# Time mixing: the modulation tiles move from the shared weight ring to three buffers of their own, loaded two tiles ahead

## The chip, the cores and the metric

The program runs on one core of a Trainium2 chip, in one launch. The metric is the device time of one execution in microseconds (us). It is given as the median of three runs.

## The reference, cut to what matters

The program is a small two-layer network on 256 positions of width 2048, all in f32. Layer 0 is RWKV-7 time mixing and an MLP; then one shared K and V are projected; layer 1 is banded attention and an MLP. Every sub-layer is normalised, scaled, shifted and gated by vectors that are computed from one condition vector `c`:

```python
mod = c @ w_ada[layer] + b_ada[layer]              # (1, 12288): 2048 x 12288 weights
sh1, sc1, gt1, sh2, sc2, gt2 = jnp.split(mod, 6, axis=-1)
h = modulate(rms_norm(x, g_mix[layer]), sh1, sc1)
y = rwkv7_time_mix(h, ...)                         # layer 0 only
x = x + gt1[:, None, :] * y
h = modulate(rms_norm(x, g_mlp[layer]), sh2, sc2)
x = x + gt2[:, None, :] * sq_relu_mlp(h, w_up[layer], w_down[layer])
```

The change concerns where the weights `w_ada` of `mod` lie while they are used. No result depends on it.

## The kernel before

**Weights.** Each 2048-wide product reads its f32 weights from HBM in tiles of 128x1024 (512 KB). `raw()` (L372) loads a tile on SyncE's queue into one of `RAW_BUFS` = 6 buffers named `raw`, which are used in turn (**the ring**): a load waits until the tile six loads back has been split. `halves()` splits a tile in two: ScalarE writes the rounded half `wH` (L382), VectorE the rest `wL` (L385); each has three buffers. TensorE multiplies by both halves (L405 to L407, or L416 and L418 in pairs). `weight_part` (L393) does the same with part of a tile.

**Modulation.** A part of `mod` (2048 numbers) is made in two halves of 16 tiles of `w_ada`. `ada_load` loads a tile; `ada_step` uses it on VectorE: the first tile of a half starts the accumulator `acc` (L458), each later one is added to it, times a number of `c` for each partition (L460). After the sixteenth, `ada_sum` adds `acc` up over the partitions by small matmuls (L482) and VectorE adds the bias (L486, `mod`). There is one buffer for `acc`. Where such a tile lies is decided here:

```python
def raw(self, src, shape=None, ada=False):
    if ada and self.ada_pool:
        pool, n = self.ada_pool
        t = pool.tile([P, HK * P], F32, tag="rada", bufs=n, name="rada")
    else:
        t = self.wp.tile([P, HK * P], F32, tag="raw", bufs=self.RAW_BUFS, name="raw")

def ada_fill(self):
    while self.ada_pool and len(self.ada_q) < self.ada_pool[1] - 1 and self.ada_load():
        pass
```

`ada_room(n)` opens a pool of n buffers named `rada` (in the MLPs n is 5, in the attention 3). While one is open, tiles of `w_ada` go there, `ada_fill` keeps n-1 of them ahead of their use, and when the room is left, `ada_drain` uses up what was loaded. Before, time mixing has no such room: there each `ada()` loads a tile into the shared ring and uses it at once.

**Time mixing.** The part of `layer_a` from L842 on runs 16 pairs of heads. A new pair begins every 8 slots, each has 36 steps (a chain of small dependent operations on all engines), and the loop over slots (L898 on) issues one step of each live pair, and two pieces of the dense products with `w_k` and `w_r` (L856 on), or of `w_o` at the end. From slot 16 on, three slots of four also call `ada()`: 111 tiles in all. Then `out_proj` multiplies by `w_o`: for each tile pair, VectorE adds the products to `x` (L955), scales the result (L557), and GpSimd adds up the squares (L524; the last is VectorE's). It reads `x` again from HBM (L941). The MLP's first products begin at once on rows that are not normalised yet, and `rstd()` (L530 on TensorE, L532 and L537 to L539 on VectorE) makes the norm beside them, which `late_norm` (L571, L572) multiplies in. L547 and L549 make the normalised rows for the rest of the MLP.

**Order.** The text of the program does not fix the order of the instructions by itself. A scheduler places each instruction on its engine by its own estimate of when its inputs are ready; an engine then runs its instructions strictly in the order that results. So a buffer more can move instructions far from the place of the edit. SyncE issues all large loads, in order, and waits at each for its buffer to be free.

Of the kernel before, what the change touches and what calls it, by code (L numbers as in the profile page):

```python
# [333 lines left out]
class Body:  # L334
# [305 lines left out]
    def layer_a(self, st, sp):  # L640
        nc, tc, d = self.nc, self.tc, self.d
# [199 lines left out]
        with ExitStack() as s1:  # L841
            pw = self.pw = s1.enter_context(tc.tile_pool(name="pw", bufs=1, reuse_waits="tile"))  # L842
            pp = self.pp = sp.enter_context(tc.tile_pool(name="ps_b", bufs=1, space=bass.MemoryType.PSUM,
                                                         reuse_waits="tile"))
            self.psm = lambda: pp.tile([P, 512], F32, tag="ms", bufs=2, name="ms")
            self.bones = pw.tile([P, P], F32R, name="bones")
            nc.scalar.copy(self.bones, self.cst("bones"))
            e01 = [pw.tile([P, 4, C + 1], F32, name=f"e01_{i}") for i in range(2)]
            self.uf = [pw.tile([P, 4, C], F32, name=f"uf_{i}") for i in range(2)]
            for e, u in zip(e01, self.uf):  # L850
                nc.vector.memset(e[:, :, 0:1], 1.0)  # L851
                nc.gpsimd.memset(u, 0.0)

            pairs = [Pair(self, j, v[:, j, :], tw, ta, tg, e01[j % 2]) for j in range(NPAIR)]

            def proj_steps(pr):  # L856
                for dst, hl in (("k", xk), ("r", xr)):
                    w = self.wnext
                    src = next(weights, None)
                    self.wnext = None if src is None else self.weight(src)  # L860
                    ps = pp.tile([P, 2 * T], F32, tag="pj", bufs=2, name="pj")[:, :T]
                    for kt in range(KT):
                        self.proj(ps, w, lambda kt: hl[:, kt, :, 0:T], (kt, kt + 1))
                        if dst == "r" and kt == 1:
                            pr.lw = pw.tile([P, 2, P], F32, tag="lw", bufs=1, name="lw")
                            nc.sync.dma_start(out=pr.lw, in_=d["lora2"][pr.j, :, 0:2])
                        if kt % 2 == 1:
                            if kt == KT - 1:
                                t = pw.tile([P, T], F32, tag=dst, bufs=2, name=dst)
                                nc.scalar.copy(t, ps)  # L870
                                setattr(pr, dst, t)
                            yield

            def out_steps():

                for n in range(8):
                    self.split(self.y_hl, n, v[:, n, :])
                sums, todo = self.o_ps, [(n, 0, HK) for n in range(8)] + [(n, HK, KT - 2) for n in range(4)]
                for n, lo, hi in todo:
                    if n % 2 == 0 and lo == 0:  # L880
                        tag = ("pj", "pj", "gr", "iv")[n // 2]
                        ps = pp.tile([P, 2 * T], F32, tag=tag, bufs=1 + (tag == "pj"), name="o")
                        sums.append(ps.rearrange("p (i t) -> p i t", i=2))
                    if lo == HK and n == 0:
                        assert all(p.done for p in pairs[:KT - 2])
                        for j in range(HK, KT - 2):
                            self.split(self.y_hl, j, v[:, j, :])
                    w = self.weight_part(d["w_o"][n], lo, hi)
                    for kt in range(lo, hi, 2):
                        self.proj(sums[n // 2][:, n % 2, :], w, lambda kt: self.y_hl[:, kt, :, 0:T],  # L890
                                  (kt, kt + 2), n % 2 == 0, False)
                        yield

            self.o_ps = []
            S, OUTS = self.SLOTS, 44
            inverts = range(Pair.EARLY, Pair.EARLY + Pair.INVERT)
            outs, done, n_out = None, 0, 0
            for slot in range(S * NPAIR + Pair.STEPS):  # L898
                live = []
                for j, pr in enumerate(pairs):  # L900
                    at = slot - S * (j + 1)
                    if 0 <= at < Pair.STEPS:
                        if at == 0:
                            pr.gen = pr.steps()
                        sums = at == Pair.STEPS - 3
                        live.append((0 if at in inverts else 1 + (at < Pair.EARLY) + 2 * sums, -at, pr))
                        pr.done = at == Pair.STEPS - 1
                last = self.last_pe()
                for _, _, pr in sorted(live, key=lambda x: x[:2]):
                    with tc.issue_after(last):  # L910
                        next(pr.gen)
                    last = self.last_pe()
                if slot < S * NPAIR:
                    if slot % S == 0:
                        dense = proj_steps(pairs[slot // S])
                    todo = 16 // S
                else:
                    if outs is None:
                        self.y_hl = self.new_hl()
                        outs = dense = out_steps()  # L920
                    todo = OUTS * (slot + 1 - S * NPAIR) // Pair.STEPS - n_out
                    n_out += todo
                with tc.issue_after(last):
                    for _ in range(todo):
                        next(dense, None)
                if slot >= 2 * S and slot % 4 < 3:
                    self.ada()
            self.fin(HK)
# [294 lines left out]


def build(arrays):
    nc = _bacc.Bacc("TRN2", target_bir_lowering=False, num_devices=1)
    d = {n: nc.dram_tensor(n, a.shape, F32, kind="ExternalInput").ap() for n, a in arrays.items()}
    d["out"] = nc.dram_tensor("out", (P, KT, T), F32, kind="ExternalOutput").ap()
    with tile.TileContext(nc) as tc, ExitStack() as ctx:
        Body(ctx, tc, d).run()  # L1230
    if not nc.is_finalized():
        nc.finalize()
    return nc
# [8 lines left out]
```

## Time and profile before

| | before |
|---|---|
| runs | 2661.66, 2654.56, 2652.42 us, median 2654.56 |
| profiled execution, first to last instruction | 2653.8 us |
| granted TensorE clock, mean | 0.993 |
| VectorE, ScalarE, GpSimd busy | 79%, 52%, 8% |

The page lists busy times, the queues, the chain of work that ended last, and the costliest groups of instructions. The time of the profiled execution itself is not listed; its span can be set beside the runs. Time mixing's pairs lie between about 185 and 710 us, `out_proj` and the start of MLP 0 between 710 and 815 us, the rest of MLP 0 up to about 1450 us. An instruction's row has line, engine, operation, and its output and inputs by the program's names; the idle time before it and what ended that idle time stand behind. TensorE's busy time has to be read with care: its matmuls are pipelined, and one of 128x256 lasts 0.28 us in a row while the next begins 0.12 us after it.

### The profile page before, as it was taken

Reading aid. Unit: us, or ns where it says so; the run is one execution under the profiler, and the core shown is the slowest. Engines: PE = TensorE matmul, PEld = TensorE weight load, DVE = VectorE, ACT = ScalarE, POOL = GpSimd, SP = SyncE. Lnnn points to the kernel's source line nnn. Section 1 sums busy time; section 2 is a strip of 40 time slices with the busy share of each in tenths; the row PEclk is TensorE's granted clock in tenths of the full one; section 3 lists DMA queues with packets and bytes.
Section 4 is the critical chain, followed back from the end, with each engine's and each line's share of the span. In section 5 each row is a group of like instructions: output and inputs, shape, how many; then the busy total and the mean of one; then the engine's idle time right before and its main releaser. Section 6 shows DMA issues by size and latency. Waiting matters only on the chain.

```text
span 2653.8 us, 59231 instructions
## 1 busy us (share of the span) xinstructions
PE 2574.9 (97%) x24108; PEld 2257.3 (85%) x24108; DVE 2089.4 (79%) x3054; ACT 1368.6 (52%) x2484; POOL 210.6 (8%) x338
## 2 busy tenths in 40 slices
PE   7999999999999999999999999999999999999997
PEld 4788888887899888888888998887898888888886
DVE  6888878878789888888888898899887556555555
ACT  3346555555456445355365554565564464453554
POOL 1002223223110000000001000000100000000002
PEclk9999999999999999999999999999999999999999
DMA  9976656565768888989888779887766555555553
GB/s 351 320 243 220 211 181 196 180 197 196 253 234 301 325 320 320 329 325 334 325 328 293 237 247 326 313 282 263 266 216 236 191 186 188 190 187 188 189 189 121
DMA packets 207664, 663.19 MB, mean 250 GB/s; under 512 B 21408, under 2 KB 55072, under 8 KB 207392
## 3 DMA queue, kind: packets, MB, share of 16 engines
q1 hardware_dynamic: 205328, 656.89, 71.7%
q8 instruction: 189, 3.10, 0.5%
q10 hardware_dynamic: 2064, 2.53, 0.3%
q14 instruction: 83, 0.68, 0.1%
HBM read 657.23 MB, written 2.10 MB: 248 GB/s over the span
## 4 chain that ended last, share of the span: by engine, by line
PE 84%; DVE 7%; issue 4%; DMA 3%; ACT 2%; POOL 1%; SPq 0%; DVEq 0%; ACTq 0%; POOLq 0%
PE pj L416 42%; PE pj L418 21%; PE pj L405 3%; PE pj L406 3%; PE pj L407 3%; DMA raw<-w_ada 2%; DVE wL L385 2%; DVE acc L460 1%; PE iv L111 1%; PE o L405 1%; PE ms L328 1%; PE o L407 0%; ACT wH L382 0%; PE o L406 0%; PE pT L1130 0%
## 5 line engine op out<-in xcount | busy, mean ns | idle before, releaser
L385 DVE TENSOR_TENSOR wL<-raw,wH 128x1024 fp32r<-128x1024 f32 x772 | 941.1, 1220 | 342.4 <-ACT wH L382 337.2
L382 ACT CAST wH<-raw 128x1024 fp32r<-128x1024 f32 x772 | 806.0, 1045 | 762.7 <-PE pj L416 590.2
L416 PE MATMUL pj<-aHL,wH 128*128 128x512 f32 x2816 | 893.3, 398 | 1.1 <-DVE x L955 1.1
L416 PE MATMUL pj<-hHL,wH 128*128 128x512 f32 x2048 | 644.7, 396 | 0.0
L418 PEld LDWEIGHTS pj<-aHL,wL 128*128 128x128 f32 x2816 | 531.7, 189 | 123.1 <-issue 0.3
L418 PE MATMUL pj<-aHL,wL 128*128 128x256 f32 x2816 | 564.1, 281 | 0.0
L418 PEld LDWEIGHTS pj<-hHL,wL 128*128 128x128 f32 x2048 | 384.5, 188 | 91.1 <-DVE wL L385 0.9
L416 PEld LDWEIGHTS pj<-aHL,wH 128*128 128x128 f32 x2816 | 432.1, 189 | 8.6 <-issue 8.3
L418 PE MATMUL pj<-hHL,wL 128*128 128x256 f32 x2048 | 402.6, 278 | 0.4 <-DVE wL L385 0.4
L460 DVE SCALAR_TENSOR_TENSOR acc<-rada,ct,acc 128x1024 f32<-128x1024 f32 x256 | 327.3, 1278 | 7.3 <-DMA rada<-w_ada 6.9
L416 PEld LDWEIGHTS pj<-hHL,wH 128*128 128x128 f32 x2048 | 312.2, 189 | 1.3 <-DVE hHL L1001 1.1
L405 PE MATMUL pj<-aHL,wH 128*128 128x256 f32 (+1 forms) x896 | 262.5, 293 | 0.0
L406 PE MATMUL pj<-aHL,wH 128*128 128x256 f32 (+1 forms) x896 | 254.2, 284 | 0.0
L407 PE MATMUL pj<-aHL,wL 128*128 128x256 f32 (+1 forms) x896 | 253.0, 282 | 0.0
L524 POOL TENSOR_TENSOR ss<-ss,sq 128x256 f32<-128x256 f32 x56 | 51.2, 915 | 1583.7 <-ACT sq L523 1583.4
L1026 DVE SCALAR_TENSOR_TENSOR x<-pj,mod,x 128x256 f32<-128x256 f32 x256 | 123.3, 482 | 64.2 <-PE pj L418 61.2
L405 PEld LDWEIGHTS pj<-aHL,wH 128*128 128x128 f32 x896 | 169.9, 190 | 4.5 <-issue 0.2
L407 PEld LDWEIGHTS pj<-aHL,wL 128*128 128x128 f32 x896 | 170.4, 190 | 0.4 <-DVE e L851 0.2
L406 PEld LDWEIGHTS pj<-aHL,wH 128*128 128x128 f32 x896 | 169.9, 190 | 0.5
L460 DVE SCALAR_TENSOR_TENSOR acc<-raw,ct,acc 128x1024 f32<-128x1024 f32 x104 | 138.0, 1327 | 17.4 <-DMA raw<-w_ada 17.2
L998 ACT ACTIVATE t<-t 128x256 f32<-128x256 f32 x112 | 46.9, 419 | 120.2 <-DVE t L970 120.2
L1001 DVE TENSOR_TENSOR hHL<-t,hHL 128x256 fp32r<-128x256 f32 x128 | 53.9, 421 | 1.7 <-ACT t L1000 1.0
(252 smaller groups left out, 2817.6 us busy)
## 6 DMA issues: line engine op xcount, KB each, us to landing
raw<-w_up SPq DMA_DIRECT2D x256, 512.0 KB, 4.0
raw<-w_down SPq DMA_DIRECT2D x256, 512.0 KB, 3.6
rada<-w_ada SPq DMA_DIRECT2D x209, 512.0 KB, 5.5
raw<-w_ada SPq DMA_DIRECT2D x111, 512.0 KB, 4.3
rada<-w_ada_kv SPq DMA_DIRECT2D x64, 512.0 KB, 6.6
rawa<-w_ada SPq DMA_DIRECT2D x32, 512.0 KB, 6.7
rawa<-w_ada_t SPq DMA_DIRECT2D x32, 512.0 KB, 7.1
raw<-w_k SPq DMA_DIRECT2D x32, 512.0 KB, 3.6
```

Of the source, the lines that this page charges most:

```text
L382: nc.scalar.copy(Hf, raw)
L385: eng.tensor_tensor(out=Lf, in0=raw, in1=Hf, op=ALU.subtract)
L405: nc.tensor.matmul(ps, H[:, i, :], a(kt)[:, 0, :], start=(first and kt == 0), stop=False)
L406: nc.tensor.matmul(ps, H[:, i, :], a(kt)[:, 1, :], start=False, stop=False)
L407: ins = nc.tensor.matmul(ps, L[:, i, :], a(kt)[:, 0, :], start=False, stop=(last and kt == KT - 1))
L416: nc.tensor.matmul(ps, w[kt // HK][0][:, kt % HK, :], a(kt), start=(kt == 0), stop=False)
L418: ins = nc.tensor.matmul(ps[:, 0, :], w[kt // HK][1][:, kt % HK, :], a(kt)[:, 0, :], start=False, stop=(kt == KT - 1))
L460: nc.vector.scalar_tensor_tensor(out=self.acc, in0=raw, scalar=ck, in1=self.acc, op0=ALU.mult, op1=ALU.add)
L524: (eng or nc.gpsimd).tensor_tensor(out=self.ss, in0=self.ss, in1=sq, op=ALU.add)
L998: nc.scalar.activation(t, t, AF.Relu)
L1001: nc.vector.tensor_tensor(out=h[:, 1, :], in0=t, in1=h[:, 0, :], op=ALU.subtract)
L1026: nc.vector.scalar_tensor_tensor(out=x, in0=ps[:, i, :], scalar=self.mods[(layer, 5)][:, n:n + 1], in1=x, op0=ALU.mult, op1=ALU.add)
```

## The change

A room of three buffers is opened around the loop over slots, and filled with two tiles at slot 12, four slots before the first `ada()`. When it is left, the two tiles that are still loaded are used: 113 tiles instead of 111. The room comes from the scratch that the build reserves for dynamic DMAs, which is set to 1024 bytes. Below L854 the line numbers are one higher than before, below L927 three higher (L955 becomes L958, L941 becomes L944).

```diff
+            s1.enter_context(self.ada_room(3))
             pairs = [Pair(self, j, v[:, j, :], tw, ta, tg, e01[j % 2]) for j in range(NPAIR)]
...
+                if slot == 2 * S - 4:
+                    self.ada_fill()
                 if slot >= 2 * S and slot % 4 < 3:
                     self.ada()
...
-    nc = _bacc.Bacc("TRN2", target_bir_lowering=False, num_devices=1)
+    nc = _bacc.Bacc("TRN2", target_bir_lowering=False, num_devices=1, dynamic_dma_scratch_size=1024)
```

GpSimd's order is the same in both programs, and TensorE's but for a batch of L482. On VectorE, ScalarE and SyncE the orders differ from shortly before the first pair up to the beginning of MLP 0; from there to the end they are equal. Three places follow; a name's number tells one buffer's use from the next.

**SyncE, where the first pairs begin.** The weights of `w_r` and `w_k` are loaded for pairs 0 and 1. Before:

```order
L372 DMA raw_2220<-w_k 128x1024
L372 DMA raw_2226<-w_k 128x1024
L372 DMA raw_2291<-w_r 128x1024
L372 DMA raw_2297<-w_r 128x1024
L372 DMA raw_2389<-w_k 128x1024
L866 DMA lw_2239<-lora2 128x256
L281 DMA lg_3772<-lora2 128x256
L372 DMA raw_2395<-w_k 128x1024
L372 DMA raw_2513<-w_r 128x1024
L372 DMA raw_2519<-w_r 128x1024
L866 DMA lw_2408<-lora2 128x256
L372 DMA raw_2538<-w_ada 128x1024
```

After:

```order
L372 DMA raw_2160<-w_r 128x1024
L372 DMA raw_2166<-w_r 128x1024
L372 DMA rada_2419<-w_ada 128x1024
L372 DMA raw_2223<-w_k 128x1024
L372 DMA rada_2421<-w_ada 128x1024
L372 DMA raw_2229<-w_k 128x1024
L372 DMA rada_2547<-w_ada 128x1024
L372 DMA raw_2294<-w_r 128x1024
L372 DMA rada_2589<-w_ada 128x1024
L372 DMA rada_2635<-w_ada 128x1024
L372 DMA raw_2300<-w_r 128x1024
```

Before, the first tile of `w_ada` is loaded behind the weights of the third projection, in the same ring. Now the tiles stand between the weights, some ten rows earlier, and take no place in the ring.

**VectorE and SyncE in out_proj.** These are the last four pairs of tiles of `w_o`. VectorE before:

```order
L557 SCALAR_TENSOR_TENSOR aHL_11661<-x_11625,gain_g_mlp0_11631,aHL_11661 128x256
L385 TENSOR_TENSOR wL_12022<-raw_12019,wH_12021 128x1024
L460 SCALAR_TENSOR_TENSOR acc_11149<-rada_12294,ct_68,acc_11149 128x1024
L955 SCALAR_TENSOR_TENSOR x_11625<-pj_11966,mod_0_2_70,x_11625 128x256
L385 TENSOR_TENSOR wL_12076<-raw_12073,wH_12075 128x1024
L955 SCALAR_TENSOR_TENSOR x_11625<-pj_11966,mod_0_2_70,x_11625 128x256
L385 TENSOR_TENSOR wL_12082<-raw_12079,wH_12081 128x1024
L557 SCALAR_TENSOR_TENSOR aHL_11661<-x_11625,gain_g_mlp0_11631,aHL_11661 128x256
L955 SCALAR_TENSOR_TENSOR x_11625<-pj_12012,mod_0_2_70,x_11625 128x256 x2
```

VectorE after:

```order
L557 SCALAR_TENSOR_TENSOR aHL_11706<-x_11670,gain_g_mlp0_11676,aHL_11706 128x256
L460 SCALAR_TENSOR_TENSOR acc_11660<-rada_12339,ct_68,acc_11660 128x1024
L385 TENSOR_TENSOR wL_12067<-raw_12064,wH_12066 128x1024
L460 SCALAR_TENSOR_TENSOR acc_11660<-rada_12341,ct_68,acc_11660 128x1024
L958 SCALAR_TENSOR_TENSOR x_11670<-pj_12011,mod_0_2_70,x_11670 128x256
L385 TENSOR_TENSOR wL_12121<-raw_12118,wH_12120 128x1024
L958 SCALAR_TENSOR_TENSOR x_11670<-pj_12011,mod_0_2_70,x_11670 128x256
L385 TENSOR_TENSOR wL_12127<-raw_12124,wH_12126 128x1024
L557 SCALAR_TENSOR_TENSOR aHL_11706<-x_11670,gain_g_mlp0_11676,aHL_11706 128x256
L460 SCALAR_TENSOR_TENSOR acc_11660<-rada_12343,ct_68,acc_11660 128x1024
L958 SCALAR_TENSOR_TENSOR x_11670<-pj_12057,mod_0_2_70,x_11670 128x256
L385 TENSOR_TENSOR wL_12167<-raw_12164,wH_12166 128x1024
```

MLP 0's room of five buffers is open here already. Before, one tile of `w_ada` is added here, the last of the seventh half, and the next comes in MLP 0. Now the additions begin at the same place and come in every few rows. The reason lies in the count: 113 is 7 times 16 and 1, so the seventh half (tiles 97 to 112) is complete within time mixing, and the next half has begun in `acc`. Before, 111 tiles left the seventh half one short; its last tile is the one above, and the next half could begin only after that half's sum (L482), which stood in MLP 0. SyncE at the same place, before:

```order
L372 DMA raw_12119<-w_o 128x1024
L372 DMA raw_12125<-w_o 128x1024
L941 DMA x_11625<-x 128x256 x2
L372 DMA rada_12294<-w_ada 128x1024
L372 DMA raw_12179<-w_o 128x1024
L372 DMA raw_12185<-w_o 128x1024
L372 DMA rada_12296<-w_ada 128x1024
L372 DMA raw_12225<-w_o 128x1024
L372 DMA rada_12298<-w_ada 128x1024
L372 DMA raw_12231<-w_o 128x1024
L372 DMA rada_12300<-w_ada 128x1024
```

SyncE after:

```order
L372 DMA raw_12164<-w_o 128x1024
L944 DMA x_11670<-x 128x256
L372 DMA rada_12339<-w_ada 128x1024
L372 DMA raw_12170<-w_o 128x1024
L372 DMA rada_12341<-w_ada 128x1024
L372 DMA raw_12224<-w_o 128x1024
L372 DMA raw_12230<-w_o 128x1024
L372 DMA rada_12343<-w_ada 128x1024
L372 DMA raw_12270<-w_o 128x1024
L372 DMA rada_12345<-w_ada 128x1024
L372 DMA raw_12276<-w_o 128x1024
L372 DMA rada_12883<-w_ada 128x1024
```

Each `rada` load stands behind a weight load, which waits for its buffer in the ring, that is for the `wL` of the tile six loads back. Before, only the first of these loads is used soon after it; now each one is.

**VectorE at the norm of MLP 0.** Before:

```order
L385 TENSOR_TENSOR wL_12392<-raw_12389,wH_12391 128x1024
L557 SCALAR_TENSOR_TENSOR aHL_11661<-x_11625,gain_g_mlp0_11631,aHL_11661 128x256
L524 TENSOR_TENSOR ss_11633<-ss_11633,sq_12280 128x256
L385 TENSOR_TENSOR wL_12398<-raw_12395,wH_12397 128x1024
L532 TENSOR_SCALAR rv_12355<-m_12353 128x256
L537 SCALAR_TENSOR_TENSOR ru_12360<-rstd_12357 128x256
L538 TENSOR_TENSOR ru_12360<-ru_12360,rv_12355 128x256
L539 SCALAR_TENSOR_TENSOR rstd_12357<-ru_12360,rstd_12357 128x256
L385 TENSOR_TENSOR wL_12468<-raw_12465,wH_12467 128x1024
```

After:

```order
L460 SCALAR_TENSOR_TENSOR acc_11660<-rada_13088,ct_68,acc_11660 128x1024
L557 SCALAR_TENSOR_TENSOR aHL_11706<-x_11670,gain_g_mlp0_11676,aHL_11706 128x256
L524 TENSOR_TENSOR ss_11678<-ss_11678,sq_12325 128x256
L385 TENSOR_TENSOR wL_12443<-raw_12440,wH_12442 128x1024
L532 TENSOR_SCALAR rv_12400<-m_12398 128x256
L460 SCALAR_TENSOR_TENSOR acc_11660<-rada_13144,ct_68,acc_11660 128x1024
L537 SCALAR_TENSOR_TENSOR ru_12405<-rstd_12402 128x256
L460 SCALAR_TENSOR_TENSOR acc_11660<-rada_13201,ct_68,acc_11660 128x1024
L538 TENSOR_TENSOR ru_12405<-ru_12405,rv_12400 128x256
L385 TENSOR_TENSOR wL_12513<-raw_12510,wH_12512 128x1024
L539 SCALAR_TENSOR_TENSOR rstd_12402<-ru_12405,rstd_12402 128x256
L460 SCALAR_TENSOR_TENSOR acc_11660<-rada_13203,ct_68,acc_11660 128x1024
```

Four additions to `acc` now stand around and inside the norm. With those of `out_proj` there are 13 additions from its last four tile pairs to the norm, where before there was one. These 13 tiles were added in MLP 0 before, between 816.6 and 849.2 us.

## The prediction

> **What bounds the kernel now.** I read the page first, then the windows by stage, then the waits within time mixing, the one buffer that the change concerns, and the chain there.
>
> ```profile
> span 2653.8 us, 59231 instructions
> PE 2574.9 (97%) x24108; PEld 2257.3 (85%) x24108; DVE 2089.4 (79%) x3054; ACT 1368.6 (52%) x2484; POOL 210.6 (8%) x338
> ...
> q1 hardware_dynamic: 205328, 656.89, 71.7%
> ```
>
> TensorE looks like the bound, but its busy time is modelled, so the question is where it loses time. The windows show engine busy times (us) in each stretch:
>
> ```profile
> core 0: us, PE busy (x) PEld busy (x) DVE busy (x) ACT busy (x) POOL busy (x), PEclk, DMA share, GB/s
> 185.00:230.00 45.00, 41.53 (x341) 40.44 (x341) 33.86 (x58) 30.78 (x58) 5.03 (x7) 0.96 0.54 178
> 230.00:300.00 70.00, 65.02 (x1445) 58.96 (x1442) 61.02 (x105) 40.76 (x105) 23.04 (x32) 1.00 0.68 214
> 400.00:500.00 100.00, 94.39 (x2111) 85.06 (x2112) 85.94 (x158) 57.15 (x159) 28.15 (x43) 1.00 0.61 198
> 600.00:710.00 110.00, 102.58 (x2106) 90.52 (x2107) 91.86 (x164) 55.10 (x158) 20.11 (x32) 0.97 0.62 206
> 860.00:1450.00 590.00, 590.00 (x3970) 515.21 (x3970) 513.03 (x591) 292.90 (x422) 5.42 (x5) 1.00 0.89 323
> ```
>
> Two regimes are seen. In MLP 0 (860 to 1450 us) TensorE is busy for all 590 us: whatever delays it ahead of that is never made up, and VectorE time saved there is worth nothing. In time mixing TensorE has gaps and VectorE is 84% to 87% busy, neither of them full: the stage lives on a chain of small steps that hand over between engines. There VectorE waits for loads of modulation tiles:
>
> ```profile
> L460 DVE SCALAR_TENSOR_TENSOR acc<-raw,ct,acc x104: 1237/1280/1910, 227.6 to 704.3; 128x1024 f32<-128x1024 f32 x104
> L458 DVE TENSOR_SCALAR acc<-raw,ct x7: 744/748/1139, 221.3 to 672.7; 128x1024 f32<-128x1024 f32 x7
> ...
>   DMA raw<-w_ada: 17.2, 19
> ```
>
> These rows are the uses of `acc` between 215 and 710 us: 111 additions, 1.28 us each at the median, and 19 of them sat behind an idle VectorE for 17.2 us in all, until their tile had landed. The other waits of VectorE and of SyncE's queue in the same stretch (total, times, longest):
>
> ```profile
> DVE u L258 <- PE iv L111: 13.8, 13, 1.7
> DVE wL L385 <- ACT wH L382: 12.6, 13, 2.2
> DVE tt L243 <- POOL u L227: 8.8, 9, 1.4
> ...
> SPq L372 <- DVE acc L460: 78.6, 45, 4.2
> SPq L372 <- DVE wL L385: 73.0, 29, 8.0
> ```
>
> So the wait for tiles is VectorE's largest single wait, but hand-overs from the other engines sum to twice as much. Is it on the path? The chain between 200 and 720 us passes through such loads, here the first and the last of ten in its list that are over 3.5 us long:
>
> ```profile
> 275.76 4.28 DMA raw<-w_ada
> ...
> 570.19 6.47 DMA raw<-w_ada
> ```
>
> About ten of the 19 waits thus end last. That is a path, not a price: without them the next-latest input decides.
>
> **The change part by part.**
>
> *The wait for tiles in time mixing.* A load takes, issue to landing:
>
> ```profile
> raw<-w_ada SPq DMA_DIRECT2D x96, 512.0 KB, 4.3
> ```
>
> The 111 additions begin between 221.3 and 704.3 us, 4.4 us apart on average. With three buffers, a tile is asked for when the addition three earlier is done, so three spacings, 13.2 us, lie between, against 4.3. But SyncE issues in order, and a tile's load can stand behind a weight load that waits for the ring, up to 8.0 us by the row above: 8.0 + 4.3 = 12.3, nearly the time there is; and additions come in bursts. I take 5 of the 17.2 us to stay and 12 to go. What a microsecond of it is worth is not shown: nothing, if a hand-over is late anyway, or a full one, on the chain's word. Ten of 19 lie on the chain, so I take a half: **6 us gained**, between 0 and 17.
>
> *The tiles moved to the front.* Before the first inverse's product (`ar` L217) VectorE now makes ten additions where it made three: 7 x 1.28 = 9 us more, in a stretch (185 to 230 us) in which it is idle for 45.0 - 33.9 = 11.1 us. They can delay a `wL` there, and relieve the stretch from 230 to 300 us, where VectorE is busy for 61 of 70. I put it at 0, with 3 us either way: seven additions at the half of a microsecond.
>
> *Two more tiles within time mixing.* One addition and one start, 1.28 + 0.75 = 2.0 us, at the end of a stretch (600 to 710) in which VectorE has 18 us idle: 0 to 2 us, I take 0.5.
>
> *The ring and the scratch.* The ring now carries weights alone, and 111 loads less pass through it, but VectorE and ScalarE hardly wait for weights. SyncE's 78.6 us behind `acc` moves to the new buffers, where the engine that waits is only a queue. The scratch is for dynamic DMAs that the program would issue in software, and q1, which carries 656.89 of the 663 MB, is of the hardware kind. Both are put at 0.
>
> *The transition to MLP 0.* Here the order, not the edit, decides. Twelve additions more stand on VectorE between the last four tile pairs of `w_o` and the norm. What room is there? The window from 742 to 781 us, the waits of VectorE in it, and its rows about the one addition that stood there:
>
> ```profile
> 742.00:781.00 39.00, 39.00 (x245) 35.10 (x244) 29.34 (x39) 19.75 (x28) 3.69 (x5) 1.00 0.79 277
> ...
> DVE wL L385 <- ACT wH L382: 3.7, 5, 1.0
> DVE acc L460 <- DMA rada<-w_ada: 2.4, 1, 2.4
> DVE x L955 <- PE pj L418: 2.3, 4, 0.7
> ...
> 746.38 1.28 DVE L460 SCALAR_TENSOR_TENSOR acc<-rada,ct,acc 128x1024 f32<-128x1024 f32 x1 [2.45 <-DMA rada<-w_ada]
> 747.58 0.48 DVE L955 SCALAR_TENSOR_TENSOR x<-pj,mod,x 128x256 f32<-128x256 f32 x1
> ```
>
> TensorE has no gap at all, VectorE 39.0 - 29.3 = 9.7 us of idle time in small pieces. An addition takes 747.58 - 746.38 = 1.20 us from start to start; twelve take 14.4. If every idle piece is filled, VectorE comes out 14.4 - 9.7 = 4.7 us late. Then the loads:
>
> ```profile
> rada<-w_ada SPq DMA_DIRECT2D x6, 512.0 KB, 6.4
> ```
>
> That is the landing time between 735 and 815 us. By the order, `rada_12343` is issued behind `raw_12230`, which takes the buffer that `wL_12067` frees. From that `wL` to the addition VectorE has one addition, two `x`, two `wL` and one L557 to do: 1.2 + 2 x 0.4 + 2 x 1.2 + 0.9 = 5.3 us, against 6.4. So VectorE waits about 1.1 us there, in order, with the next `wL` behind it. Counted like this, nine of the 13 additions have less than 6.8 us of work between (6.4 and the issue); I take five such waits, 5.5 us, between none and nine. Late by 4.7 + 5.5 = 10, between 4.7 and 14.
>
> Does TensorE feel it? Two places:
>
> ```profile
> 775.22 0.42 DVE L524 TENSOR_TENSOR ss<-ss,sq 128x256 f32<-128x256 f32 x1
> ...
> 789.27 2.36 DVE L385 TENSOR_TENSOR wL<-raw,wH 128x1024 fp32r<-128x1024 f32 x2
> ...
> 776.88 0.59 PE L530 MATMUL m<-ss,csts 128*128 128x256 f32 x2
> ...
> 790.55 0.39 PE L407 MATMUL pj<-aHL,wL 128*128 128x258 f32 x1
> ```
>
> The sum of squares was done at 775.64 and used by TensorE at 776.88: 1.2 us to spare. The first of the two `wL` from 789.27 was done at about 790.5 and used at 790.55: nothing to spare. So nearly the whole lag becomes a gap of TensorE: **9 us lost**, between 3.5 (4.7 less 1.2) and 14. The twelve additions taken out of 816 to 849 us give nothing back, since TensorE had no gap there either.
>
> The page "SBUF — State Buffer" of the Trainium skill, in "Who interferes with whom", says that a VectorE operation with two inputs in SBUF and a GpSimd operation that reads SBUF lock each other out for a whole instruction. `acc` is such an operation, and among the new additions stand GpSimd's L524. The trace agrees as far as it goes: in time mixing, where GpSimd was busy for 28 us of 100 (400 to 500), an addition lasted up to 1.91 us, 1.28 at the median. By the rule, additions that meet an L524 would take up to 0.63 us longer each, and the loss would be some 2 us greater (an estimate); by the median alone it is as above.
>
> **Sum.** 2653.8 - 6 + 0 + 0.5 + 9 = 2657.3 us of span. The runs' median lies 0.8 us above the span of the profiled execution, so I add it: **2658 us**, 0.1% above 2654.56. A measurement of this kernel can tell about 0.3%, 8 us, from no change: below 2646.6 is faster, above 2662.5 slower.
>
> **The rivals.**
>
> *The waits are worth their full length, and the transition is soft.* For it: the chain runs through ten of these loads, and VectorE is 87% busy in the early pairs, where little else can be late. Against it: hand-overs of 13.8, 12.6 and 8.8 us remain beside them. Then 17 are gained and 4.7 lost: 2654.6 - 17 + 4.7 = 2642 us.
>
> *VectorE starves TensorE ahead of MLP 0 (slower).* In time mixing the hand-overs take up what the tiles leave (gain 0 to 2), and most of the additions in `out_proj` wait for their loads, so that a lag of 14 us stands where the norm is due. It decides from the point where the loads land later than 5.3 us after issue, since that is the work in front of an addition; the 6.4 above speaks for it. Against it: waits that fall together with idle pieces are paid once. 2654.6 - 1 + 14 = 2668 us.
>
> *The change moves waits and nothing else.* The scheduler now puts each addition where it expects its tile to land, so additions wait as before, only later ones; and the lag at the transition stays within the slack. Then 2654.6 - 1 + 2 = 2656 us. Against it is the place with no slack at 790.55.
>
> **How the numbers follow.** The forecast has 0.45, of which 0.06 lies above 2662.5; the full gain 0.22, of which 0.02 ends within 0.3%; the starved TensorE 0.25, all but 0.01 of it slower; the moved waits 0.08. That makes faster 0.20, same 0.50, slower 0.30. The likeliest case's own range is 2652 to 2664. The range of 2644 to 2668 reaches into both outer cases, to the lower end of the unknown gain and to the upper end of the lag, and leaves about 0.1 out on each side.
>
> **What would show it.** In time mixing the wait of `acc` for its DMA should fall from 17.2 us to about 5, the additions bear `rada` for `raw`, and the last pair should end some 6 us earlier, about 704 for 710 us. From 742 to 790 us VectorE should have next to no idle time but new waits of `acc` for `rada`, and TensorE gaps of about 9 us in all, where it has none now, at L530 or behind a `wL`. From 860 us on, both kernels should take the same time, to a microsecond or two. I am wrong if TensorE has no gap around the norm (then the scheduler's additions fitted the idle time), if time mixing ends later than before (then the early additions delay the pairs' chain), or if it ends more than 12 us earlier (then the waits were worth their full length).

## The result, and the profile after

The change makes the kernel slower: 2670.43 us at the median (2668.89 to 2671.27, six runs) against 2655.95 us before (2652.27 to 2663.40, six runs on the same chip). The ratio is 1.0048, with an interval of 1.0034 to 1.0062. That is 14.5 us more, where 3.5 more were forecast, and 2.4 us beyond the range. The head of the page after:

```profile
span 2667.4 us, 59218 instructions
PE 2582.2 (97%) x24108; PEld 2259.0 (85%) x24108; DVE 2089.0 (78%) x3054; ACT 1366.7 (51%) x2484; POOL 207.7 (8%) x338
```

VectorE does the same work (2089 us) in a span that is 13.6 us longer. So VectorE's work has not become dearer; something waits more. What the change was made for has happened. The waits of VectorE between 215 and 710 us, after:

```profile
DVE wL L385 <- ACT wH L382: 19.9, 17, 2.2
DVE u L258 <- PE iv L111: 19.4, 18, 2.3
DVE tt L243 <- POOL u L227: 15.5, 15, 1.4
DVE acc L460 <- DMA rada<-w_ada: 4.4, 8, 1.1
```

The wait for tiles fell from 17.2 to 4.4 us, and the hand-overs from the other engines grew. The windows after, at the places that the prediction named:

```profile
185.00:230.00 45.00, 38.13 (x321) 37.18 (x319) 39.02 (x60) 30.56 (x56) 4.40 (x7) 1.00 0.79 273
230.00:300.00 70.00, 64.07 (x1255) 57.99 (x1256) 50.84 (x91) 39.92 (x100) 23.98 (x31) 0.95 0.50 160
...
742.00:781.00 39.00, 37.29 (x220) 32.16 (x218) 34.90 (x39) 16.50 (x24) 6.40 (x6) 1.00 0.86 303
781.00:815.00 34.00, 29.27 (x207) 28.68 (x208) 30.98 (x56) 17.98 (x33) 0.00 (x0) 0.85 0.76 259
...
860.00:1450.00 590.00, 590.00 (x3968) 514.94 (x3967) 507.43 (x586) 294.24 (x425) 1.89 (x3) 1.00 0.89 319
```

The prediction shows most of these windows as they were before. The one from 781 to 815 us was:

```profile
781.00:815.00 34.00, 34.00 (x341) 33.77 (x340) 32.81 (x66) 23.82 (x42) 0.00 (x0) 1.00 0.56 179
```

Two places have got worse. In the first 45 us of the pairs TensorE is busy for 38.1 us instead of 41.5, while VectorE has more to do (39.0 for 33.9). And around the norm TensorE now has gaps, 1.7 us in one window and 4.7 us in the next, and in the second its granted clock is 0.85 where it was 1.00. From 860 us on it has none, as before.

How much each place costs can be read more sharply. TensorE's order is nearly the same in both programs, so the n-th matmul of a line in one can be set beside the n-th in the other. This table, worked out from the rows of both traces, has the median difference of 20 such neighbours: how many us later TensorE is than before at the same work. The head is the time in the kernel before.

| kernel | 195 | 230 | 260 | 290 | 450 | 600 | 705 | 725 | 772 | 779 | 793 | 850 | 2500 |
|---|---|---|---|---|---|---|---|---|---|---|---|---|---|
| the change | 0.5 | 5.7 | 8.7 | 7.8 | 4.0 | 2.2 | 1.0 | 1.6 | 2.4 | 8.9 | 12.8 | 12.1 | 13.5 |

It reads like a bill. The first pairs lose 8.2 us (0.5 to 8.7). The later pairs win 7.7 us (8.7 to 1.0). The norm and what leads to it lose 11.1 us (1.0 to 12.1). The remaining 1.4 us come behind 1500 us, where the orders are equal; other kernels below gain or lose as much there, and it was not followed up.

TensorE's waits from 700 to 900 us after the change name the second place (before there was a single one, of 2.1 us, at the first `wL` of `out_proj`):

```profile
PE m L530 <- DVE ss L524: 4.3, 1, 4.3
PE o L407 <- DVE wL L385: 2.3, 2, 1.6
PE pj L405 <- ACT wH L382: 1.0, 1, 1.0
PE pj L407 <- DVE wL L385: 1.0, 1, 1.0
```

These are the two places that the prediction had found with 1.2 us to spare and with nothing to spare. VectorE's and TensorE's rows there, after:

```profile
778.58 1.28 DVE L460 SCALAR_TENSOR_TENSOR acc<-rada,ct,acc 128x1024 f32<-128x1024 f32 x1 [1.02 <-DMA rada<-w_ada]
...
783.29 0.42 DVE L524 TENSOR_TENSOR ss<-ss,sq 128x256 f32<-128x256 f32 x1
...
791.08 0.42 DVE L539 SCALAR_TENSOR_TENSOR rstd<-ru,rstd 128x256 f32<-128x256 f32 x1
...
783.77 1.22 PE L530 MATMUL m<-ss,csts 128*128 128x256 f32 x2 [4.30 <-DVE ss L524]
```

The sum of squares is 8.1 us later than before (775.22), and TensorE stands still for 4.3 us until it is there. The norm is 11.0 us later. Before it was:

```profile
780.04 0.43 DVE L539 SCALAR_TENSOR_TENSOR rstd<-ru,rstd 128x256 f32<-128x256 f32 x1
```

The gaps are not the whole loss. The three waits in the list above that lie here (L530, and L405 and L407 of `pj`) come to 6.3 us, against 10.4 us in the table from 772 to 793. Behind the gap at L530, TensorE's matmuls begin 0.22 us apart until 788.4, where 0.12 is usual:

```profile
785.00 0.42 PE L406 MATMUL pj<-aHL,wH 128*128 128x258 f32 x1
785.22 0.42 PE L407 MATMUL pj<-aHL,wL 128*128 128x258 f32 x1
```

From 772 to 820 us the granted clock was 0.89, before 1.00. The other 4 us are about what that takes (an estimate: 0.11 of 48 us is 5.3 us, a part of it while TensorE waited anyway).

The first place the prediction had passed over. VectorE's rows in the first pair, before:

```profile
212.38 0.42 DVE L125 TENSOR_TENSOR sq<-s,sq 128x256 fp32r<-128x256 f32 x1
212.75 1.23 DVE L385 TENSOR_TENSOR wL<-raw,wH 128x1024 fp32r<-128x1024 f32 x1
215.15 0.69 DVE L138 TENSOR_SCALAR s<-ms 128x512 f32<-128x512 f32 x1 [1.18 <-PE ms L134]
215.76 1.21 DVE L385 TENSOR_TENSOR wL<-raw,wH 128x1024 fp32r<-128x1024 f32 x1
217.84 0.69 DVE L149 TENSOR_TENSOR_SCAN s<-csts,s 128x256 f32<-128x256 f32 x1 [0.86 <-ACT s L143]
219.09 1.23 DVE L385 TENSOR_TENSOR wL<-raw,wH 128x1024 fp32r<-128x1024 f32 x1 [0.56 <-ACT wH L382]
...
221.26 0.97 DVE L458 TENSOR_SCALAR acc<-raw,ct 128x1024 f32<-128x1024 f32 x1
...
225.02 0.47 DVE L178 SCALAR_TENSOR_TENSOR s<-r,vecs,s 128x256 f32<-128x256 f32 x1
```

After:

```profile
211.74 0.41 DVE L125 TENSOR_TENSOR sq<-s,sq 128x256 fp32r<-128x256 f32 x1
212.07 1.27 DVE L460 SCALAR_TENSOR_TENSOR acc<-rada,ct,acc 128x1024 f32<-128x1024 f32 x1
213.47 1.22 DVE L385 TENSOR_TENSOR wL<-raw,wH 128x1024 fp32r<-128x1024 f32 x1
214.61 2.60 DVE L460 SCALAR_TENSOR_TENSOR acc<-rada,ct,acc 128x1024 f32<-128x1024 f32 x2
217.13 0.68 DVE L138 TENSOR_SCALAR s<-ms 128x512 f32<-128x512 f32 x1
217.73 1.22 DVE L385 TENSOR_TENSOR wL<-raw,wH 128x1024 fp32r<-128x1024 f32 x1
218.86 1.28 DVE L460 SCALAR_TENSOR_TENSOR acc<-rada,ct,acc 128x1024 f32<-128x1024 f32 x1
...
221.35 0.68 DVE L149 TENSOR_TENSOR_SCAN s<-csts,s 128x256 f32<-128x256 f32 x1
221.95 1.26 DVE L460 SCALAR_TENSOR_TENSOR acc<-rada,ct,acc 128x1024 f32<-128x1024 f32 x1
...
229.04 0.47 DVE L178 SCALAR_TENSOR_TENSOR s<-r,vecs,s 128x256 f32<-128x256 f32 x1
```

L125, L138, L149 and L178 are steps of one pair's chain. Before, it took 12.6 us from L125 to L178 (212.38 to 225.02), now 17.3 us (211.74 to 229.04). Five additions stand between, 6.0 us of work from start to start; so do one `wL` and two small steps (L174, L175) more than before, 1.8 us, and the start of `acc` (L458, 0.9 us) is gone from there. That is 6.9 us more, and the idle pieces that it could fill were 1.18, 0.86 and 0.56 us, 2.6 us in all. The 4.3 us that are left over are nearly the 4.7 us that were measured. The first inverse's product (`ar` L217) begins 5.2 us later (236.26 for 231.06). How the loss grows from there to 8.2 us at 260 was not taken apart; one part may be the granted clock, 0.92 from 230 to 275 us where it was 1.00.

### The profile page after: what moved, and what is told of

It reads as the page before. It is cut to its first block, busy times and chain, and to the rows that moved or that the text cites. A ratio compares the mean times of both kernels' runs of the same rounds, so it can differ in the third digit from the quotient of the medians.

```text
span 2667.4 us, 59218 instructions
## 1 busy us (share of the span) xinstructions
PE 2582.2 (97%) x24108; PEld 2259.0 (85%) x24108; DVE 2089.0 (78%) x3054; ACT 1366.7 (51%) x2484; POOL 207.7 (8%) x338
## 4 chain that ended last, share of the span: by engine, by line
PE 83%; DVE 7%; issue 3%; DMA 3%; ACT 2%; POOL 1%; DVEq 0%; SPq 0%; ACTq 0%; POOLq 0%
PE pj L416 41%; PE pj L418 21%; PE pj L405 3%; PE pj L406 3%; PE pj L407 3%; DVE wL L385 2%; DMA rada<-w_ada 2%; DVE acc L460 2%; PE iv L111 1%; PE gr L105 1%; PE ms L328 1%; ACT wH L382 1%; PE o L405 0%; PE m L698 0%; PE pT L1133 0%
## 5 line engine op out<-in xcount | busy, mean ns | idle before, releaser
L460 DVE SCALAR_TENSOR_TENSOR acc<-rada,ct,acc 128x1024 f32<-128x1024 f32 x360 | 462.0, 1283 | 17.8 <-DMA rada<-w_ada 17.3
L405 PE MATMUL pj<-aHL,wH 128*128 128x256 f32 (+1 forms) x896 | 264.4, 295 | 1.0 <-ACT wH L382 1.0
L407 PE MATMUL pj<-aHL,wL 128*128 128x256 f32 (+1 forms) x896 | 254.6, 284 | 2.9 <-DVE e L851 1.9
L405 PEld LDWEIGHTS pj<-aHL,wH 128*128 128x128 f32 x896 | 171.7, 192 | 5.9 <-ACT wH L382 1.2
L524 POOL TENSOR_TENSOR ss<-ss,sq 128x256 f32<-128x256 f32 x56 | 51.6, 921 | 1594.2 <-ACT sq L523 1593.9
L407 PEld LDWEIGHTS pj<-aHL,wL 128*128 128x128 f32 x896 | 172.2, 192 | 3.4 <-DVE e L851 2.1
L1001 ACT ACTIVATE t<-t 128x256 f32<-128x256 f32 x112 | 46.9, 418 | 124.7 <-DVE t L973 124.7
L1003 ACT ACTIVATE t<-t 128x256 f32<-128x256 f32 x128 | 53.3, 417 | 3.4
```

Of the source, the lines that this page charges most:

```text
L405: nc.tensor.matmul(ps, H[:, i, :], a(kt)[:, 0, :], start=(first and kt == 0), stop=False)
L407: ins = nc.tensor.matmul(ps, L[:, i, :], a(kt)[:, 0, :], start=False, stop=(last and kt == KT - 1))
L460: nc.vector.scalar_tensor_tensor(out=self.acc, in0=raw, scalar=ck, in1=self.acc, op0=ALU.mult, op1=ALU.add)
L524: (eng or nc.gpsimd).tensor_tensor(out=self.ss, in0=self.ss, in1=sq, op=ALU.add)
L1003: nc.scalar.activation(t, t, AF.Square)
```

## The experiments

Every kernel was timed against the kernel before on its own chip. The table has all results; where a kernel stays behind or ahead, the columns say where TensorE lost or won it.

| kernel | median us | ratio to before | interval | 260 | 290 | 600 | 725 | 793 | 2500 |
|---|---|---|---|---|---|---|---|---|---|
| the change | 2670.4 | 1.0048 | 1.0034 to 1.0062 | 8.7 | 7.8 | 2.2 | 1.6 | 12.8 | 13.5 |
| tiles111 | 2660.1 | 1.0013 | 1.0004 to 1.0021 | 11.9 | 10.9 | 4.5 | 5.8 | 5.8 | 6.0 |
| norm_held | 2663.0 | 1.0012 | 1.0003 to 1.0021 | 11.3 | 10.4 | 4.0 | 4.9 | 5.0 | 5.6 |
| before_113 | 2670.1 | 1.0057 | 1.0042 to 1.0072 | 1.8 | 1.8 | 2.8 | 4.5 | 13.8 | 14.1 |
| front_held | 2668.9 | 1.0051 | 1.0036 to 1.0065 | 5.3 | 9.1 | 2.2 | 1.7 | 9.7 | 9.2 |
| both | 2656.0 | 1.0000 | 0.9991 to 1.0010 | 4.4 | 8.2 | -0.8 | 2.3 | 2.2 | 3.2 |
| scratch_only | 2656.1 | 0.9994 | 0.9985 to 1.0003 | 1.2 | 1.2 | -1.4 | -2.3 | -2.2 | -1.5 |
| room_from_40 | 2650.7 | 0.9971 | 0.9960 to 0.9983 | 0.4 | 0.4 | -4.7 | -3.3 | -3.3 | -2.3 |
| room_from_64 | 2652.3 | 0.9985 | 0.9976 to 0.9994 | 1.9 | 1.9 | -5.9 | -9.3 | -9.4 | -7.0 |
| room_to_40 | 2661.8 | 1.0014 | 1.0005 to 1.0022 | 12.4 | 11.5 | 11.1 | 4.2 | 4.2 | 5.3 |
| from_40_113 | 2662.6 | 1.0015 | 1.0005 to 1.0025 | -0.1 | -0.2 | -7.1 | -5.1 | 4.8 | 6.8 |
| two_buffers | 2659.2 | 1.0003 | 0.9990 to 1.0016 | 1.3 | 2.2 | 6.8 | 5.9 | 5.9 | 6.4 |
| early_loads | 2652.0 | 0.9976 | 0.9966 to 0.9985 | 2.6 | 3.1 | -6.7 | -6.0 | -6.0 | -5.9 |

The columns are from one profiled execution each, and they vary between profiles even where two programs have the same order of VectorE and ScalarE. scratch_only, with the order of the kernel before throughout, has 1.2 at 260 and -2.3 at 725; tiles111, with the order of the change up to 705 us, stands at 11.9 for 8.7 at 260 and at 6.7 for 1.0 at 705. So a difference of 5 us in one column proves little by itself, and the ratios, from 5 to 12 runs each, have the last word. What repeats can be trusted: where the tiles are used early, the first pairs lose 8.2 to 10.3 us (195 to 260) in four profiles.

### The norm

**tiles111** leaves out the last two calls in time mixing:

```diff
-                if slot >= 2 * S and slot % 4 < 3:
+                if slot >= 2 * S and slot % 4 < 3 and slot < S * NPAIR + Pair.STEPS - 3:
                     self.ada()
```

> The change, but time mixing uses 111 tiles as before (the last two calls of ada() are left out; the drain uses the two tiles that are loaded), so that in the order only one addition stands between the last tile pairs of w_o and the norm. Theory (the twelve additions there cost TensorE about 10 us): about 2660 us, TensorE without a gap at L530, the wait of the sum of squares gone. Rival (the gap comes from time mixing's late end or from the tiles in the early MLP room, not from the count): still 2668 to 2671 us.

It came out at 2660.1 us, as the theory said, and nothing is lost any more between 725 and 793 us. **norm_held** keeps the 113 tiles, but holds the additions behind VectorE's earlier instructions:

```diff
             if q or f >= RAW - 2:
-                self.ada_tick(layer)
+                with ExitStack() as held:
+                    if layer == 0 and q == 0:
+                        held.enter_context(tc.issue_after(self.last_of(nc.vector)))
+                    self.ada_tick(layer)
```

> The change with all 113 tiles, but the additions that MLP 0's first part asks for are held behind the VectorE instructions written before them, so that none of them stands between w_o's last pairs and the norm. Theory (the position, not the count itself, makes the loss): as tiles111, 2658 to 2662 us. Rival (two more tiles or the earlier sum cost it): 2668 to 2671 us.

Ratio 1.0012, like tiles111 (1.0013), and 1 us above the expected range. TensorE's waits from 715 to 860 us there are:

```profile
PE o L407 <- DVE wL L385: 2.3, 2, 1.5
PE o L406 <- DVE aHL L581: 0.5, 1, 0.5
```

The wait at L530 is gone though the count is 113. The wait of 2.3 us that is left is that of `out_proj`'s `wL`, as the kernel before has it with 2.1 us. So the count only opens the way; the place of the additions makes the loss. **before_113** adds the two tiles to the kernel before, which has no room there (`self.ada(2)` in the last slot):

> The kernel before, with no room, but with two more tiles at the end of time mixing (113 as in the change). Eleven additions then stand around the norm of MLP 0. Theory (the count makes the loss): 2664 to 2668 us, with a gap of TensorE at L530. Rival (the loss needs the room): 2655 to 2658 us.

It is as slow as the change, 2670.1 us, 2 us above what was expected: it loses 9.3 us between 725 and 793 and some 4 us ahead of that. Its granted clock was 1.00 from 772 to 820 us, and TensorE stood idle for 8.0 us there: the loss does not need the lower clock either. The loss at the norm needs neither room nor early loads.

### The first pairs

**front_held** holds the additions of slots 16 to 31:

```diff
-                    self.ada()
+                    with ExitStack() as held:
+                        if slot < 4 * S:
+                            held.enter_context(tc.issue_after(self.last_of(nc.vector)))
+                        self.ada()
```

> The change, but the additions of slots 16 to 31 are held behind the last VectorE instruction that the program wrote before them, so that none stands ahead of the first pair's ar; three of the tiles are still loaded early, among the first weights. Theory (the early additions on VectorE delay the first pairs by 7 to 8 us): about 2663 us, TensorE at 255 us no more than 2 us later than before the change. Rival 1 (the early loads delay the first weights): still about 2670 us. Rival 2 (the additions that were done early are what made the later pairs faster): the 7 us come back later in time mixing, about 2670 us.

> Both edits, 111 tiles and the early additions held. Theory (two separate losses of 7 and 10 us beside a gain of 7 us from the waits): 2650 to 2654 us, a few us below the kernel before. Rival (the gain within time mixing was only work moved to the front): 2656 to 2660 us.

Both are misses. front_held stayed slow; `both` was level with the kernel before, as the rival said. The table shows that this is not the rival's reason: up to 230 us TensorE loses nothing (0.1 us from 195 to 230 in front_held, 5.2 in the change), but by 290 us it is 7.0 us late all the same (2.1 to 9.1), and then it wins 6.9 us up to 600 as the change does. The loss was moved, not taken away. VectorE's rows in front_held show where to:

```profile
253.53 1.28 DVE L460 SCALAR_TENSOR_TENSOR acc<-rada,ct,acc 128x1024 f32<-128x1024 f32 x1
254.75 0.29 DVE L258 TENSOR_TENSOR u<-u,iv 128x128 f32<-128x128 f32 x1
254.95 1.28 DVE L460 SCALAR_TENSOR_TENSOR acc<-rada,ct,acc 128x1024 f32<-128x1024 f32 x1
...
256.49 1.27 DVE L460 SCALAR_TENSOR_TENSOR acc<-rada,ct,acc 128x1024 f32<-128x1024 f32 x1
257.68 0.30 DVE L243 STREAM_TRANSPOSE tt<-u 128x128 f32<-128x128 f32 x1
```

`u` and `tt` are two neighbouring steps of the loop that inverts a pair's matrix, and TensorE (`iv`) waits for `tt`. Two additions now stand between them, 2.5 us, and once more two between the steps at 241.2 and 244.4; in the kernel before it is never more than one up to 300 us. So the question had to be put without moving additions to new places. **room_from_40** opens the room at once but uses it from slot 40, so that VectorE's order ahead of that is the one of before; **room_from_64** does so from slot 64; **room_to_40** is the reverse:

```diff
             s1.enter_context(self.ada_room(3))
+            room, self.ada_pool = self.ada_pool, None
...
-                if slot == 2 * S - 4:
+                if slot == 40:
+                    self.ada_pool = room
                     self.ada_fill()
```

```diff
+                if slot == 40:
+                    self.ada_drain(2)
+                    self.ada_pool = None
```

All three have 111 tiles.

> The change with 111 tiles, but the room is used only from slot 40 on (before that the tiles go through the shared ring as before), so that VectorE's order up to the fourth pair is that of the kernel before. Theory (the room costs 7 to 9 us in the first pairs and wins 7 to 9 us in the later ones, each by itself): 2648 to 2651 us, TensorE at 290 us level with before and some 7 us earlier at 650 us. Rival (the later pairs only catch up what the first ones lost, because something else paces them): 2655 to 2658 us, level with before throughout.

> As room_from_40, from slot 64 on, three pairs later. Theory: a part of the later gain goes, 2650 to 2653 us. Rival: 2655 to 2658 us as well.

> The change with 111 tiles, but the room is used only up to slot 40, then its two tiles are used up and the shared ring serves as before. Theory (separate loss and gain): the first pairs lose 7 to 9 us and little comes back, 2662 to 2665 us. Rival (later pairs catch up anyhow): 2656 to 2659 us.

room_from_40 is level with before at 290 us (0.4) and ahead by 4.7 us at 600: 2650.7 us, faster than both kernels. It differs from tiles111 in the use of the room before slot 40 alone, and the two ratios, 0.9971 and 1.0013, lie 0.42% apart, 11 us: that is what the early use costs where the room serves later too. room_from_64 wins as well; its columns go further than room_from_40's, but its profile is the fastest of its eleven runs and the other the slowest of its six. room_to_40 loses 10 us in the first pairs (12.4, with 2.1 at 195) and keeps them up to 600; at 2661.8 us it lies just below the expected range, because 7 us come back between 600 and 725 us. Most of that is the clock of this profile: granted 1.00 in that stretch, where the kernel before had 0.96, which is 5 us of 125. So the gain can be had without the loss. But the two do not simply add up: the early use alone costs 0.14% (room_to_40), the late use alone wins 0.29% (room_from_40), and both together, in tiles111, cost 0.13% where the sum would win 0.15%, outside the intervals. How much of the gain is left once the first pairs are late stays open.

**early_loads** asks whether the first pairs lose by the additions or by the loads. To room_from_40 it adds eight loads at slot 12 that nothing uses:

```diff
+                if slot == 2 * S - 4:
+                    self.ada_pool = room
+                    for i in range(8):
+                        self.raw(self.ada_src(0, 2)[0][i * P:(i + 1) * P, 0:HK * P], ada=True)
+                    self.ada_pool = None
```

> room_from_40 with eight more loads of w_ada tiles at slot 12 into the room, which nothing uses; on SyncE they stand among the first weights nearly where the change has its tiles, while VectorE's order stays that of room_from_40. Theory (the first pairs lose by the additions on VectorE): as room_from_40, 2649 to 2653 us, TensorE within 1 us of it at 260 us. Rival (they lose by the loads, which delay the first weights): 7 to 9 us more, 2657 to 2660 us.

The window shows that the loads were there, 0.83 of the DMA engines' time against 0.79 in the change:

```profile
185.00:230.00 45.00, 40.88 (x329) 39.77 (x329) 32.89 (x55) 30.29 (x57) 4.44 (x7) 0.96 0.83 279
```

The time is 2652.0 us, ratio 0.9976, as room_from_40 within the intervals. TensorE is 2.6 us late at 260 us, more than the 1 us that was expected and far less than the change. But kernels with the same order there and no such loads have up to 1.9 (room_from_64), so a cost of the loads is not shown. In room_from_40 itself three loads into the room are issued as early (185.7 to 194.8 us). The loss follows VectorE's order.

### The gain, and the scratch

**two_buffers** is room_from_40 with `ada_room(2)`, one tile ahead:

> room_from_40 with two buffers, loaded one tile ahead, 111 tiles. Theory (the gain is the wait for tiles, and one ahead hides only a part of it): more waits of acc for its load than the 5.5 us of room_from_40, 2652 to 2656 us. Rival (the gain comes from the ring that carries weights alone): as room_from_40, 2650 us.

The waits for tiles between 215 and 710 us, room_from_40 first (up to slot 40 the tiles lie in the ring, and are named `raw`):

```profile
DVE acc L460 <- DMA rada<-w_ada: 5.5, 6, 2.1
...
DVE acc L460 <- DMA raw<-w_ada: 3.2, 4, 1.9
```

two_buffers:

```profile
DVE acc L460 <- DMA rada<-w_ada: 24.4, 27, 2.3
DVE acc L460 <- DMA raw<-w_ada: 3.8, 5, 1.8
```

With the ring just as free, 19.5 us more of waits (28.2 for 8.7) go with 9.2 us more of time at 725 us (5.9 for -3.3): 0.47 us for each. The ratios, 0.32% apart, say 8.5 us and 0.44. The median, 2659.2 us, is 3 us above the expected range; one tile ahead waits more than none ahead did (17.2).

**scratch_only** is the kernel before with the smaller scratch:

> The kernel before with the smaller scratch alone. Both theories: no change, 2654 to 2658 us; if it were slower, a part of the loss would be the scratch's.

No difference. **from_40_113** puts the two tiles back into room_from_40:

> room_from_40 with all 113 tiles, so that the twelve additions stand around the norm again. Theory (the losses add up): 10 us more than room_from_40's 2650.7, 2659 to 2663 us, the gap of TensorE at L530 back. Rival (the loss at the norm needs the late end of time mixing that the first pairs cause): 2650 to 2654 us.

2662.6 us, 12 us above room_from_40, 9.9 of them between 725 and 793 us, though time mixing ends 5 us early in this profile. The losses add up.

## Why the prediction was wrong, point by point

- **The wait in time mixing: right in the waits, and in their worth as far as is shown.** 12 of 17.2 us were to go, and 12.8 went; a microsecond was to be worth a half, and two_buffers shows 0.47. Forecast 6 us gained, measured 7.7 from 260 to 705 us; 5.2 and 7.3 in tiles111 and norm_held, which have the same order there. That all of it comes from the waits is not shown, since late pairs may also catch up; room_from_40, which was not late, wins 0.29%, 7.7 us, with 8.5 us less of waits, which is nearer to a whole microsecond for each (0.17% to 0.40% by the interval). And time mixing did not end 6 us earlier: at 705 us TensorE is 1.0 us later than before (6.7 and 4.0 in tiles111 and norm_held), the prediction's own sign that the early additions delay the pairs.
- **The tiles moved to the front: the step that failed.** The prediction put it "at 0, with 3 us either way", on the ground that VectorE was idle for 11.1 us between 185 and 230 us. It cost 8.2 us in the profile, and 11 us by the ratios of tiles111 and room_from_40; without the later use, in room_to_40, 0.14%, 3.7 us. The seven additions were counted rightly, and so was the window's idle time; but it was taken as cover for work that stood elsewhere in the window. Between L125 and L178 of the first pair, where five additions went, there were 2.6 us of it. front_held, room_from_40 and early_loads show that the loss follows VectorE's order; that each of its microseconds comes from an addition in a pair's chain is read from the rows, not tried one by one.
- **Two more tiles in time mixing: not shown.** 0.5 was forecast; between 705 and 725 us TensorE loses 0.6, far less than two profiles differ by.
- **Ring and scratch at 0: right for the scratch**, by scratch_only. No run tries the ring alone; two_buffers, whose ring is as free as room_from_40's, was level with the kernel before.
- **The transition: right in place, and in mechanism but for the clock.** Forecast were five waits of 5.5 us for `rada`, VectorE 10 us late and TensorE 9 us, at L530 or behind a `wL`. Measured: seven waits, 5.4 us, the norm 11.0 us late (of which 1.6 to 2.4 were there before), TensorE 10.4 us from 772 to 793 and 9.7 to 850. Only 6.3 us of these were gaps; the rest goes with the lower granted clock behind them, of which the prediction says nothing. Twelve additions were counted ahead of the norm; the rows have nine more than before ahead of the sum of squares and eleven ahead of L539. The lock between VectorE and GpSimd, for which the prediction cited the page "SBUF — State Buffer" of the Trainium skill, was to add some 2 us to the additions, and it did not: they took 1.27 to 1.29 us each. It fell on the other side. The two L524 of GpSimd that began while an addition ran took 1.48 and 1.93 us, where the others took 0.73 to 0.78 and all seven took 0.74 before; the last of them was done at 774.7 us, long before VectorE's L524 at 783.29.
- **The sum.** With 8.2 for 0 in the one term, 3.5 becomes 11.7 us; 13.6 were measured in the span. The rival that ended slower came near the time (2668) for half a reason and by luck: its transition of 14 us was too dear (11.1 measured from 705 us on), and its gain of 1 us in time mixing is near the truth only because a loss of 8.2 and a gain of 7.7 nearly cancel there; it, too, knew nothing of the first pairs.

The chance of slower was 0.30. It should have been the likeliest case: two places were known where additions were to stand ahead of what TensorE needs, and in both their cost was set against idle time summed over a whole window.

## What to carry to other kernels

A buffer that lets a load start early also lets the scheduler put its consumer early. Look first at where the consumers now stand in the order, and ahead of which chain, since work off the path can cost its full length once it stands in an in-order queue ahead of work on it. Idle time covers added work only if it lies at that place of the chain: add it up between the two instructions, not over a window. And when one part of a change wins and another loses, limit it to the stretch where it wins: from slot 40 on, with the count of tiles of before, the room was worth 0.3%.

## What the runs showed that was not expected

One buffer more or less turns the sign of the change in waits: with two buffers VectorE waited 28.2 us for tiles, more than in the shared ring of six (17.2), with three 8.7. And a kernel that is late through waits can lose once more behind them: after the 4.3 us gap at L530 the granted clock was lower, and some 4 us more went (the estimate above). And eight loads of 512 KB that nothing uses, put ahead of the first pairs, cost no time that the comparison shows (0.9976 with them, 0.9971 without), although the DMA engines were busy for 0.83 of that window instead of 0.63.
